# Neighbourhood attention by blocks of 16 columns in a two-block transformer kernel on one Trainium2 core

## The chip, the cores and the metric

The kernel runs on one core of a Trainium2 chip. The metric is the device time of one execution, in microseconds. The two kernels of this case are timed on the same chip, and a ratio of their times is read with its interval.

## What is computed

The reference is two transformer blocks. The change touches one part of the first: the attention layer over 512 latent tokens, seen as a grid of 8 rows by 64 columns, with 256 context tokens beside them. Its first half, neighbourhood attention, has 8 heads of 64 numbers. A latent query attends to the keys of a window of 8 rows by 16 columns around it, with a bias by relative position, and to all 256 context keys; since the grid has 8 rows, the window holds all of them, and only the columns slide. A context query attends to the context keys alone. Cut to what matters:

```python
row0 = clip(q_row - 4, 0, rows - 8)
col0 = clip(q_col - 8, 0, 64 - 16)
s_win = einsum('bqhd,bqkhd->bhqk', q, k[window]) * scale + rpb[:, rel_r, rel_c]
s_ctx = einsum('bqhd,bkhd->bhqk', q, k_ctx) * scale
p = softmax(concatenate([s_win, s_ctx], -1))
o = p[..., :128] @ v[window] + p[..., 128:] @ v_ctx
```

The result is gated by silu(ga), joined with that of a grouped-query attention (GQA), and multiplied by `w_out`. The rest of both blocks is the same in both kernels.

## The kernel before

The program is written once, in order, for all engines; a scheduler then lays out each engine's list, following the written order as a priority, and an engine runs its list in order. Work that is written as filler is mixed into the lists of the stage around it.

In `attn_layer` the projections come first. `gemm_T` gives an output turned (features on partitions, tokens along the row: `qaT`, `kaT`, `gaT`), in blocks of 256 features; `gemm_N` gives it natural (128 tokens on partitions), and makes `va`, six tiles of 128 tokens. Every product there is three products of rounded parts (lines 114 to 116).

Then comes the neighbourhood stage. `na_bias` loads `E`, for each query column the biases of all 64 key columns by 15 row distances, with eight loads, and adds a mask of -1e30 outside the window (line 463: the first two heads on VectorE, the others on GpSimd). `attend` runs over 4 head pairs `pr`, 3 query groups `qg` (two of 256 latent queries, one of context queries), 2 heads `p` and 2 tiles `i` of 128 queries, which are two grid rows. For a latent tile, `Softmax.probs` multiplies the queries with all 512 latent keys and with the 256 context keys (line 405, in two PSUM banks of the four `mm`), adds the bias and takes the maximum in one VectorE operation (line 414), reduces the second part (line 410), and runs two exponentials on ScalarE (line 420). `Softmax.transpose` turns the six tiles of 128 probabilities on TensorE (line 439), three to a bank of `tr`, and ScalarE and VectorE copy them out (lines 444 and 442). For a query group the six turned tiles are multiplied with `va` (line 751), the two heads innermost, each with its own half of the output's partitions. Lines 757 to 764 and `split` (199, 200) scale, gate and store the result. A matmul of 32-bit numbers stands in the trace as two passes.

`fill_a`, written ahead of head pair 0, is filler of this stage: it streams 32 pieces of 512 KB of modulation weights through two buffers and multiplies them (lines 333, 345, 369) in the one bank `fx`. The stage after it is the GQA, with filler `fill_b`.

Of the kernel before, what the change touches and what calls it, by code (L numbers as in the profile page):

```python
# [10 lines left out]
F32 = mybir.dt.float32  # L11
F32R = mybir.dt.float32r
AF = mybir.ActivationFunctionType
OP = mybir.AluOpType
# [434 lines left out]
NB = 64 * 15  # L449


def na_bias(b, pool, rpb, namask):


    nc = b.nc
    E = pool.tile([128, 8, 64, 15], F32, name="E")
    n = rpb.shape[1]
    for h in range(0, 8, 2):
        for a in range(2):
            src = bass.AP(tensor=rpb.tensor, offset=rpb.offset + h * n + 1 - a, ap=[[15, 64], [n, 2], [1, NB]])  # L460
            nc.sync.dma_start(E[64 * a:64 * a + 64, h:h + 2].rearrange("p h k x -> p h (k x)"), src)
        e = E[:, h:h + 2]
        (nc.gpsimd if h else nc.vector).tensor_tensor(e, e, namask[:, None, :, None].to_broadcast([128, 2, 64, 15]), op=OP.add)
    return E

# [61 lines left out]
def gemm_N(b, w, c0, ncols, hh, hl, nt, evac, tags=("mm", "ac"), done=None):  # L527
# [4 lines left out]
    ahead = []  # L532

# [42 lines left out]
def attn_layer(b, I, A, B, gates, modulate, consts, open_x, fill_a, fill_b):  # L576
# [29 lines left out]
    with b.banks(mm=4, tr=2, ac=2), tc.tile_pool(name="attn_h", bufs=1, side="right") as hp, \  # L606
# [21 lines left out]
        gemm_T(b, w_in, 0, 512, hh, hl, segs, put(qaT, lambda d, p: nc.scalar.activation(d, p, AF.Copy, scale=0.125)),  # L628
# [3 lines left out]
        qS, kS = gq.tile([128, 8, T], F32R, name="qS"), gq.tile([128, 2, 2, T], F32R, name="kS")  # L632
# [11 lines left out]
        for j in range(2):  # L644
            for cs in range(2):
# [82 lines left out]
    def attend(sm, pr, qT, kT, v, g2, bias, okt):  # L728


        for qg in range(3):
# [5 lines left out]
            for p in range(2):  # L737
                keys = lambda a, e: [k[:, a:e] for k in kT(p)]
                for i in range(2):
                    t = qg * 2 + i  # L740
                    q = qT(p)[:, t * 128:t * 128 + 128]
                    if lat and bias:
                        pieces = [(keys(0, 512), bias(2 * pr + p, t)), (keys(512, 768), None)]
                    else:
                        pieces = [(keys(0 if lat else 512, 768), None)]
                    pp = sm.probs(q, pieces, nk * 128, ri[:, i, p:p + 1])
# [5 lines left out]
            t = sm.work.tile([128, 256], F32, name="ot")  # L752
            sl = slice(qg * 256, qg * 256 + 256)

            rp = b.psum(256, sm.tags[1])
            rb = sm.work.tile([128, 4, 64], F32, name="ot")
            nc.gpsimd.tensor_scalar(rb, ri.rearrange("q i p -> q (i p)")[:, :, None].to_broadcast([128, 4, 64]), 1.0, 0.0,
                                    op0=OP.mult, op1=OP.add)
            for i in range(2):
                nc.tensor.transpose(rp[:, i * 128:i * 128 + 128],  # L760
                                    rb[:, 2 * i:2 * i + 2].rearrange("q p d -> q (p d)"), b.ident)
            nc.vector.tensor_mul(t, rp, g2[:, sl])
            nc.vector.scalar_tensor_tensor(t, o, 0.5, t, op0=OP.mult, op1=OP.mult)
            b.split(t, o_hi[okt // 4][:, okt % 4, sl], o_lo[okt // 4][:, okt % 4, sl])

    with b.banks(mm=4, tr=2, ac=1, fx=1), tc.tile_pool(name="na_e", bufs=1, side="right") as ep, \
            tc.tile_pool(name="na_w", bufs=2, side="right") as work:
        E = na_bias(b, ep, I["na_rpbP"], I["k_namask"])
        sm = Softmax(b, work)
        for pr in range(4):  # L770
            if pr == 0:
                fill_a("fx")
            attend(sm, pr, lambda p: qaT[64 * p:64 * p + 64, pr], lambda p: [kaT[64 * p:64 * p + 64, pr]],
                   lambda p, j: va[:, j, (2 * pr + p) * 64:(2 * pr + p) * 64 + 64], gaT[:, pr],
# [1753 lines left out]
```

## Time and profile before

| | us |
|---|---|
| median of 3 runs (2924.91 to 2933.57) | 2927.23 |
| the profiled execution | 2929.68 |
| its span, first to last instruction | 2927.9 |
| TensorE busy in the span | 2719.4 (93%) |
| VectorE / ScalarE / GpSimd busy | 1516.5 / 1035.1 / 511.9 |

The profile is of one execution. All durations below come from it; it lies 2.4 us above the median. PE is TensorE, PEld its weight loads, DVE VectorE, ACT ScalarE, POOL GpSimd. L405 is line 405. The windows view gives for a stretch (us from the span's start) its length, then for PE, PEld, DVE, ACT and POOL the busy time and the number of instructions that start in it, then TensorE's granted clock (1.00 is 2.4 GHz, 0.50 is 1.2 GHz), the DMA engines' busy share and the GB/s. A group of instructions stands as line, engine, operation, output<-inputs, shapes and count, then busy time in us and the mean of one in ns, then the idle time ahead of it and what ended that. For a matmul "64\*128" is rows by columns of the array that are in use and "64x512" the operand that streams through. The neighbourhood stage is the stretch from 281 to 462 us.

### The profile page before, as it was taken

To read this page: it belongs to the slowest core of one execution; us is meant where nothing else is said; L and a number is where in the kernel's file an instruction comes from. 1 tells how busy PE (TensorE), PEld (TensorE's weight loads), DVE (VectorE), ACT (ScalarE), POOL (GpSimd) and SP (SyncE) were. 2 spreads that over 40 slices of the span, in tenths; PEclk is the share of its full clock that TensorE was granted. 3 is DMA by queue.
4 is the path that set the end of the run, shared out by engine and by line. 5 is a ranking of instruction groups with operands and counts; after the bars stand their busy time and mean duration, and the time that the engine had idled before them with its cause. 6 is when DMAs were issued, how large, how long until landed. Compare 5 with 4: busy or idle time off the path is not lost. (4 is left out here: it accounts for less than half of the span.)

```text
span 2927.9 us, 43748 instructions
## 1 busy us (share of the span) xinstructions
PE 2719.4 (93%) x16874; PEld 2133.7 (73%) x16874; DVE 1516.5 (52%) x3218; ACT 1035.1 (35%) x2157; POOL 511.9 (17%) x803
## 2 busy tenths in 40 slices
PE   8998998989989889887999998999999998899998
PEld 5987445669767666667888877676878556888887
DVE  4144557645477788685434237662234445533423
ACT  3122336534444444213323224432224543322322
POOL 1011100221343332332000001311011333200000
PEclk9999899989889899988999998999999999999999
DMA  6112441132223322424333223223444114233322
GB/s 222 62 59 65 140 123 43 53 115 90 83 82 118 93 84 82 163 79 141 101 95 100 94 85 105 83 91 112 121 119 124 54 46 146 91 94 101 94 101 87
DMA packets 248796, 288.31 MB, mean 98 GB/s; under 512 B 16983, under 2 KB 196650, under 8 KB 248588
## 3 DMA queue, kind: packets, MB, share of 16 engines
q1 hardware_dynamic: 237068, 248.96, 27.2%
q0 software_dynamic: 10704, 33.41, 3.7%
q8 instruction: 133, 2.18, 0.3%
q10 hardware_dynamic: 816, 3.15, 0.3%
q14 instruction: 75, 0.61, 0.1%
HBM read 248.73 MB, written 35.68 MB: 97 GB/s over the span
## 5 line engine op out<-in xcount | busy, mean ns | idle before, releaser
L109 DVE TENSOR_TENSOR wlo<-wraw,whi 128x512 fp32r<-128x512 f32 (+1 forms) x390 | 368.6, 946 | 694.3 <-ACT whi L108 688.1
L108 ACT ACTIVATE whi<-wraw 128x512 fp32r<-128x512 f32 (+1 forms) x390 | 323.7, 831 | 809.6 <-PE mm L115 225.8
L114 PE MATMUL mm<-hh,whi 128*128 128x512 f32 (+1 forms) x992 | 371.8, 376 | 0.8 <-ACT hh L178 0.7
L115 PE MATMUL mm<-hl,whi 128*128 128x512 f32 (+1 forms) x992 | 371.8, 375 | 0.0
L116 PE MATMUL mm<-hh,wlo 128*128 128x512 f32 (+1 forms) x992 | 371.5, 375 | 0.1
L114 PEld LDWEIGHTS mm<-hh,whi 128*128 128x128 f32 x992 | 188.6, 191 | 34.2 <-ACT hh L178 1.3
L116 PEld LDWEIGHTS mm<-hh,wlo 128*128 128x128 f32 x992 | 188.4, 190 | 34.1 <-DVE wlo L109 1.2
L115 PEld LDWEIGHTS mm<-hl,whi 128*128 128x128 f32 x992 | 188.6, 190 | 32.2
L114 PE MATMUL mm<-whi,mh 128*128 128x512 f32 (+1 forms) x480 | 172.3, 360 | 1.4 <-DVE th L2138 1.4
L115 PE MATMUL mm<-wlo,mh 128*128 128x512 f32 (+1 forms) x480 | 173.2, 361 | 0.1
L116 PE MATMUL mm<-whi,ml 128*128 128x512 f32 (+1 forms) x480 | 172.8, 360 | 0.0
L114 PE MATMUL gt<-hh,whi 128*128 128x512 f32 (+1 forms) x320 | 128.4, 401 | 7.6 <-ACT whi L108 6.1
L116 PE MATMUL gt<-hh,wlo 128*128 128x512 f32 (+1 forms) x320 | 128.6, 402 | 0.6 <-DVE wlo L109 0.6
L115 PE MATMUL gt<-hl,whi 128*128 128x512 f32 (+1 forms) x320 | 127.8, 399 | 0.0
L283 POOL TENSOR_TENSOR ss<-sq 128x1 f32<-128x1 f32 x8 | 1.6, 201 | 708.0 <-ACT th L277 708.0
L114 PE MATMUL mm<-lath,whi 128*128 128x512 f32 (+1 forms) x280 | 117.7, 421 | 0.1
L116 PE MATMUL mm<-lath,wlo 128*128 128x512 f32 (+1 forms) x280 | 115.5, 413 | 0.6 <-DVE wlo L109 0.6
L115 PE MATMUL mm<-latl,whi 128*128 128x512 f32 (+1 forms) x280 | 115.2, 412 | 0.4 <-DVE latl L179 0.4
L114 PEld LDWEIGHTS mm<-whi,mh 128*128 128x128 f32 x480 | 89.9, 188 | 15.8 <-DVE th L2138 1.8
L115 PEld LDWEIGHTS mm<-wlo,mh 128*128 128x128 f32 x480 | 90.1, 188 | 14.6 <-DVE wlo L109 0.8
L116 PEld LDWEIGHTS mm<-whi,ml 128*128 128x128 f32 x480 | 90.1, 188 | 13.6
L439 PEld LDWEIGHTS tr<-ident,s 128*128 128x128 f32 x448 | 53.2, 148 | 52.6 <-ACT s L420 23.6
(716 smaller groups left out, 6157.0 us busy)
## 6 DMA issues: line engine op xcount, KB each, us to landing
wraw<-in_ffn_w_gate SPq DMA_DIRECT2D x44, 512.0 KB, 3.6
wraw<-in_ffn_w_up SPq DMA_DIRECT2D x44, 512.0 KB, 3.6
wraw<-in_ffn_w_down SPq DMA_DIRECT2D x44, 512.0 KB, 3.2
wraw<-in_w_in SPq DMA_DIRECT2D x60, 256.0 KB, 2.9
wraw<-in_rec_w_in SPq DMA_DIRECT2D x58, 256.0 KB, 2.8
wraw<-in_attn_w_in SPq DMA_DIRECT2D x26, 512.0 KB, 3.6
ada_w<-in_rec_ada_w SPq DMA_DIRECT2D x24, 512.0 KB, 3.9
wraw<-in_w_branch_gate SPq DMA_DIRECT2D x48, 256.0 KB, 3.0
```

Source lines behind the costliest of these rows:

```text
L108: nc.scalar.activation(hi, raw, AF.Copy)
L109: self.weng.tensor_sub(lo, raw, hi.bitcast(F32))
L114: mm(out, lh, rh, start=start, stop=False)
L115: mm(out, lh, rl, start=False, stop=False)
L116: mm(out, ll, rh, start=False, stop=stop)
L283: nc.gpsimd.tensor_add(ss, sq[:, i, 0:1], sq[:, i, 1:2])
L439: nc.tensor.transpose(t[:, j * 128:j * 128 + 128], p[:, (g + j) * 128:(g + j) * 128 + 128], b.ident)
```

## The change

The neighbourhood attention is cut another way. A query tile is a block of 16 columns by 8 rows instead of two grid rows, so its latent keys are a slice of columns of the grid: 32 columns (256 keys) for the two inner blocks and 24 columns (192 keys) for the two outer ones, instead of all 512. For this

- the evacuation of `qaT` writes the queries in the order block, column, row;
- the values are projected by `gemm_T` into `vT`, evacuated in groups of 8 columns by 8 rows, and turned by 24 transposes into `va` (`turn_v`, between the two halves of the gate's projection); `vT` stands in the buffer of `kS`, which is made after it;
- `E` is 8 row distances by 80 columns for each query and head, prepared ahead with the mask inside, loaded by eight loads; the mask's constant and the four additions are gone;
- the scores of the window and of the context go into one bank a head, and the products of the two heads alternate (`scores`);
- a tile has four tiles of probabilities to turn instead of six, in one bank; ScalarE copies two and VectorE two;
- the product with the values runs over four key tiles of 128 queries, instead of over six of 256;
- the gating reads `gaT` and writes the outputs in the grid's order, through views with a stride of 64 numbers.

The GQA keeps `attend`, of which the gating is now a function. Though the change's name also speaks of the sparse attention, no line of that is in the diff.

```diff
-NB = 64 * 15
+NA_E = 80
...
-    E = pool.tile([128, 8, 64, 15], F32, name="E")
...
+    E = pool.tile([128, 8, 8, NA_E], F32, name="E")
+    for h in range(8):
+        src = bass.AP(tensor=rpb.tensor, offset=rpb.offset + h * 16 * 15 * NA_E + 7 * NA_E,
+                      ap=[[15 * NA_E, 16], [-NA_E, 8], [1, 8 * NA_E]])
+        nc.sync.dma_start(E[:, h].rearrange("p r x -> p (r x)"), src)
...
+        def queries(j, ps):
+            d = qaT[:, j]
+            by = lambda x, how: x.rearrange(f"p ({how}) -> p r b c", b=4, c=16)
+            nc.scalar.activation(by(d[:, 0:S], "b c r"), by(ps[0], "r b c"), AF.Copy, scale=0.125)
+            nc.scalar.activation(d[:, S:T], ps[1], AF.Copy, scale=0.125)
...
-        gemm_N(b, w_in, 1024, 512, hh, hl, 6,
-               lambda c, i, p: nc.vector.tensor_copy(va[:, i, c * 256:c * 256 + 256], p))
-        gemm_T(b, w_in, 1536, 512, hh, hl, segs, put(gaT, lambda d, p: silu2(b, work, d, p)))
+        def values(j, ps):
+            v = vT[:, j]
+            grid = lambda x: x.rearrange("p (r c) -> p r c", c=64)
+            by = lambda x: grid(x)[:, :, 8:56].rearrange("p r (g c) -> p g r c", c=8)
+            nc.scalar.activation(v[:, 128:512].rearrange("p (g r c) -> p g r c", g=6, r=8), by(ps[0]), AF.Copy)
+            nc.vector.tensor_copy(v[:, 0:128].rearrange("p (g r c) -> p g r c", g=2, r=8),
+                                  grid(ps[0]).rearrange("p r (g c) -> p g r c", c=8)[:, ::7])
+            nc.scalar.activation(v[:, 512:768], ps[1], AF.Copy)
+        def turn_v(j):
+            v = vT[:, j]
+            for i, n in ((0, 4), (4, 2)):
+                p = b.psum(n * 128, "tr")
+                for m in range(n):
+                    nc.tensor.transpose(p[:, m * 128:m * 128 + 128], v[:, (i + m) * 128:(i + m) * 128 + 128], b.ident)
+                nc.vector.tensor_copy(va[:, i:i + n, j * 128:j * 128 + 128], p.rearrange("p (m f) -> p m f", m=n))
+        gemm_T(b, w_in, 1024, 512, hh, hl, segs, values)
+        gemm_T(b, w_in, 1536, 256, hh, hl, segs, put(gaT, lambda d, p: silu2(b, work, d, p)))
+        for j in range(4):
+            turn_v(j)
+        kS = gq.tile([128, 2, 2, T], F32R, name="kS")
+        gemm_T(b, w_in, 1536 + 256, 256, hh, hl, segs, put(gaT[:, 2:4], lambda d, p: silu2(b, work, d, p)))
...
+    def attend_na(sm, pr, E):
+        def scores(i):
+            ps = [b.psum(512, "mm") for _ in range(2)]
+            parts = [(256, [kaT[hs, pr, S:T] for hs in heads])]
+            if i < 4:
+                cols = slice(max(16 * i - 8, 0), min(16 * i + 24, 64))
+                n = 8 * (cols.stop - cols.start)
+                parts.insert(0, (n, [grid(kaT[hs, pr, 0:S])[:, :, cols] for hs in heads]))
+            o = 0
+            for n, ks in parts:
+                for p in range(2):
+                    nc.tensor.matmul(ps[p][:, o:o + n], qaT[heads[p], pr, 128 * i:128 * i + 128], ks[p], start=True, stop=True)
+                o += n
+            return ps, o
+        def probs(p, m, i, h, ri):
...
+            nc.vector.tensor_tensor_reduce(rows(z), rows(p), E[:, h, :, e0:e0 + w // 8], 1.0, NEG, OP.add, OP.max, mx[:, 0:1])
+            nc.vector.tensor_reduce(mx[:, 1:2], p[:, w:m], op=OP.max, axis=AX.X)
+            nc.vector.tensor_reduce(nm, mx, op=OP.max, axis=AX.X, negate=True)
+            nc.scalar.activation(s[:, 0:w].rearrange("p (g r c) -> p g r c", r=8, c=8),
+                                 z[:, 0:w].rearrange("p (r g c) -> p g r c", r=8, c=8), AF.Exp, bias=nm, accum_out=sums[:, 0:1])
+            nc.scalar.activation(s[:, w:m], p[:, w:m], AF.Exp, bias=nm, accum_out=sums[:, 1:2])
...
+            for x in range(2):
+                i = 2 * qg + x
+                ps, m = scores(i)
+                at = [0, m - 384] if lat else []
+                at += [m - 256, m - 128]
+                for p in range(2):
+                    s = probs(ps[p], m, i, 2 * pr + p, ri[:, x, p:p + 1])
+                    t = b.psum(512, "tr")
+                    for j, a in enumerate(at):
+                        nc.tensor.transpose(t[:, j * 128:j * 128 + 128], s[:, a:a + 128], b.ident)
+                    tv = t.rearrange("p (a b) -> p a b", b=128)
+                    xs = slice(128 * x, 128 * x + 128)
+                    nc.scalar.activation(pT[:, p, 0:2, xs], tv[:, 0:2], AF.Copy)
+                    if lat:
+                        nc.vector.tensor_copy(pT[:, p, 2:4, xs], tv[:, 2:4])
+            o = b.psum(256, "ac")
...
+                for j, (n, rows) in enumerate(tiles):
+                    for p in range(2):
+                        h = 2 * pr + p
+                        nc.tensor.matmul(o[heads[p], xs], va[rows, n, h * 64:h * 64 + 64], pT[rows, p, j, xs],
+                                         start=j == 0, stop=j == nk - 1)
+            gated(sm, o, ri, cut(gaT[:, pr]), cut(o_hi[0][:, pr]), cut(o_lo[0][:, pr]))
```

## Rows read from the trace of the kernel before

**Rows 1.** the page: the span and the busy time of TensorE.

```profile
span 2927.9 us, 43748 instructions
PE 2719.4 (93%) x16874; PEld 2133.7 (73%) x16874; DVE 1516.5 (52%) x3218; ACT 1035.1 (35%) x2157; POOL 511.9 (17%) x803
```

**Rows 2.** the windows view, by stretch: columns as in the section on the profile before.

```profile
281.00:292.00 11.00, 3.44 (x9) 1.91 (x10) 5.05 (x7) 0.38 (x1) 0.63 (x1) 0.81 0.91 222
292.00:312.00 20.00, 20.00 (x56) 9.84 (x56) 9.54 (x33) 7.85 (x24) 10.77 (x4) 0.51 0.70 167
312.00:462.00 150.00, 147.97 (x732) 66.21 (x728) 91.19 (x282) 58.79 (x182) 6.28 (x14) 1.00 0.35 108
466.00:600.00 134.00, 118.51 (x721) 83.71 (x722) 100.04 (x228) 80.74 (x183) 20.42 (x24) 0.96 0.19 63
```

**Rows 3.** groups of instructions by form, TensorE, 312 to 462 us.

```profile
L439 PE MATMUL tr<-ident,s 128*128 128x128 f32 x198 | 32.9, 285 | 0.7 <-DVE ot L762 0.4 <-ACT s L420 0.3
L751 PE MATMUL ac<-pT,va 128*64 128x256 f32 x202 | 32.5, 390 | 0.0
L405 PE MATMUL mm<-kaT,qaT 64*128 64x512 f32 x52 | 28.7, 631 | 0.0
L405 PE MATMUL mm<-kaT,qaT 64*128 64x256 f32 x86 | 27.9, 421 | 0.4 <-DVE mx L414 0.4
L760 PE MATMUL tr<-ident,ot 128*128 128x128 f32 x22 | 5.0, 303 | 0.2 <-POOL ot L757 0.2
L333 PE MATMUL fx<-ada_w,ada_cs 128*32 128x512 f32 x128 | 29.5, 605 | 0.7 <-DMA ada_w<-in_rec_ada_w 0.7
L369 PE MATMUL fx<-xt,k_sel 128*128 128x512 f32 x8 | 4.4, 632 | 0.0
L345 PE MATMUL fx<-k_sel,xt 128*128 128x2 f32 x32 | 4.2, 254 | 0.0
L369 PE MATMUL fx<-xt,k_sel 128*1 128x512 f32 x4 | 2.0, 591 | 0.0
```

**Rows 4.** TensorE: groups by form 435.24 to 435.30 us; three timeline pieces (start us, us, what).

```profile
L405 PE MATMUL mm<-kaT,qaT 64*128 64x512 f32 x1 | 0.7, 693 | 0.0
...
L405 PE MATMUL mm<-kaT,qaT 64*128 64x256 f32 x1 | 0.5, 480 | 0.0
...
435.24 0.70 PE L405 MATMUL mm<-kaT,qaT 64*128 64x256 f32 x2
...
444.81 0.44 PE L751 MATMUL ac<-pT,va 128*64 128x256 f32 x2
...
2392.58 1.09 PE L1923 MATMUL ac<-pT,vn 128*64 128x128 f32 x8
```

**Rows 5.** groups by form, VectorE and ScalarE, 312 to 462 us; last, line 1900 (ns min/median/max).

```profile
L414 DVE CUSTOM_DVE_ANT_1 s<-mm,E 128x512 f32<-128x512 f32 x26 | 27.4, 1052 | 7.8 <-PE mm L405 7.6
L442 DVE COPY pT<-tr 128x384 f32<-128x384 f32 x28 | 15.5, 552 | 6.5 <-PE tr L439 6.0
L410 DVE TENSOR_REDUCE mx<-mm 128x1 f32<-128x256 f32 x27 | 11.3, 419 | 2.8 <-PE mm L405 2.2
L420 ACT ACTIVATE s<-mm,nm 128x256 f32<-128x256 f32 x43 | 19.9, 464 | 2.6 <-DVE nm L408 2.1 <-DVE ri L425 0.5
L1900 DVE CUSTOM_DVE_ANT_0 s<-mm,E x96: 132/348/692, 2223.8 to 2431.4; 128x128 f32<-128x128 f32 x16, 128x256 f32<-128x256 f32 x16, 128x384 f32<-128x384 f32 x16, 128x512 f32<-128x512 f32 x16
```

**Rows 6.** timeline, the first biased tile; last, landing of the loads of E.

```profile
287.98 2.16 DVE L463 TENSOR_TENSOR E<-E,k_namask 128x1920 f32<-128x1920 f32 x1 [1.96 <-DMA E<-in_na_rpbP]
...
291.38 2.04 PE L405 MATMUL mm<-kaT,qaT 64*128 64x512 f32 x2 [7.21 <-DVE mx L414]
...
DMA to landing us min/median/max: 6.7/7.5/8.3
```

**Rows 7.** the windows view again, two blocks of 256 features: keys, then values.

```profile
85.36:102.04 16.68, 16.68 (x98) 14.76 (x97) 2.45 (x2) 3.86 (x6) 0.00 (x0) 1.00 0.21 64
127.78:145.06 17.28, 17.28 (x145) 17.28 (x144) 4.72 (x8) 2.12 (x2) 0.00 (x0) 1.00 0.20 62
```

More of the change, by code (lines that the diff above doesn't have):

```diff
@@ L446, in transpose, with na_bias @@
             g += m
-NB = 64 * 15
-def na_bias(b, pool, rpb, namask):
+NA_E = 80
+def na_bias(b, pool, rpb):
     nc = b.nc
-    E = pool.tile([128, 8, 64, 15], F32, name="E")
[L457 to L463, printed above, removed]
+    E = pool.tile([128, 8, 8, NA_E], F32, name="E")
[3 more added lines that the diff above has]
+        nc.sync.dma_start(E[:, h].rearrange("p r x -> p (r x)"), src)
     return E
@@ L627, in attn_layer @@
         modulate(work, place, ("tr", "tr"), 1)
[L628 removed]
+        def queries(j, ps):
[3 more added lines that the diff above has]
+            nc.scalar.activation(d[:, S:T], ps[1], AF.Copy, scale=0.125)
+        gemm_T(b, w_in, 0, 512, hh, hl, segs, queries,
                mid=lambda: half(1), pre=pre)
         consts()
[L632 removed]
+        qS, vT = gq.tile([128, 8, T], F32R, name="qS"), gq.tile([128, 4, T], F32, name="kS")
         kaT, gaT = na.tile([128, 4, T], F32, name="kaT"), na.tile([128, 4, T], F32, name="gaT")
@@ L726, in attn_layer, with attend @@
     open_o()
-    def attend(sm, pr, qT, kT, v, g2, bias, okt):
+    def attend(sm, pr, qT, kT, v, g2, okt):
         for qg in range(3):
@@ L741, in attend @@
                     q = qT(p)[:, t * 128:t * 128 + 128]
[L742 to L746, printed above, removed]
+                    pp = sm.probs(q, [(keys(0 if lat else 512, 768), None)], nk * 128, ri[:, i, p:p + 1])
                     sm.transpose(pp, pT[:, p, :, i * 128:i * 128 + 128], nk)
@@ L759, in attend @@
[L759 to L764, printed above, removed]
+            gated(sm, o, ri, g2[:, sl], o_hi[okt // 4][:, okt % 4, sl], o_lo[okt // 4][:, okt % 4, sl])
@@ new lines, in gated @@
+    def gated(sm, o, ri, g2, hi, lo):
+        rp = b.psum(256, sm.tags[1])
+        rb = sm.work.tile([128, 4, 64], F32, name="ot")
+        nc.gpsimd.tensor_scalar(rb, ri.rearrange("q i p -> q (i p)")[:, :, None].to_broadcast([128, 4, 64]), 1.0, 0.0,
+                                op0=OP.mult, op1=OP.add)
+        for i in range(2):
+            nc.tensor.transpose(rp[:, i * 128:i * 128 + 128],
+                                rb[:, 2 * i:2 * i + 2].rearrange("q p d -> q (p d)"), b.ident)
+        t = sm.work.tile([128, 256], F32, name="ot")
+        like = lambda x: x if len(g2.shape) == 2 else x.rearrange("p (b c r) -> p b c r", b=2, r=8)
+        nc.vector.tensor_mul(like(t), like(rp), g2)
+        nc.vector.scalar_tensor_tensor(t, o, 0.5, t, op0=OP.mult, op1=OP.mult)
+        b.split(like(t), hi, lo)
@@ L772, in attn_layer @@
                 fill_a("fx")
[L773 to L775 removed]
+            attend_na(sm, pr, E)
     right.close()
@@ L2408, in consts @@
     C["k_rope"] = np.stack([cos, sin], 0).reshape(2, 4, 128, 64).transpose(2, 0, 1, 3)
-    m = np.full((2, 64, 64), NEG)
-    for q in range(64):
-        c0 = min(max(q - 8, 0), 48)
-        m[:, q, 48 - c0:64 - c0] = 0
-    C["k_namask"] = m.reshape(128, 64)
     p = np.arange(128)
@@ L2469, in layout @@
     rpb = a["na_rpb"][0]
-    R["na_rpbP"] = np.zeros((8, 127 * 15 + 1), rpb.dtype)
-    R["na_rpbP"][:, 48 * 15:79 * 15] = rpb.transpose(0, 2, 1)[:, ::-1].reshape(8, -1)
+    parts = []
+    for q0, k0, n in ((16, 8, 32), (0, 0, 24), (48, 40, 24)):
+        t = np.full((8, 16, 15, n), NEG, rpb.dtype)
+        for q in range(q0, q0 + 16):
+            first = min(max(q - 8, 0), 48)
+            for k in range(max(k0, first), min(k0 + n, first + 16)):
+                t[:, q - q0, :, k - k0] = rpb[:, :, k - q + 15]
+        parts.append(t)
+    R["na_rpbP"] = np.concatenate(parts, 3).reshape(8, -1)
     R["ccols"] = np.stack([a["c"][0], a["c_ctx"]], -1).reshape(8, 128, 2).transpose(1, 0, 2)
```

47 lines of the change are left out of this document (37 added, 10 removed).

## The prediction

> **What bounds the kernel now.** The page comes first: TensorE is busy for 2719.4 of 2927.9 us [rows 1], so what counts is TensorE's own time, stage by stage. The windows view gives it for the neighbourhood stage, 281 to 462 us, 181 us long [rows 2]. Its body, 312 to 462, is TensorE's: 147.97 of 150 us busy at the full clock of 2.4 GHz, while VectorE is busy for 91.19 (61%) and ScalarE for 58.79. Its head is not: in 281 to 292 TensorE works 3.44 of 11 us, and after that idle stretch it runs at the lower clock (0.51) for 20 us, though it has work all the time. The gap ends when the first bias is masked and used: the mask takes VectorE 2.16 us after the load has landed, and TensorE's next scores wait 7.21 us for VectorE [rows 6]. So a pass taken from TensorE in the body is worth its time, as long as the others keep up. In the next stage, the GQA, they don't quite: VectorE is busy for 100.04 of 134 us (75%), and TensorE only for 118.51 (88%) [rows 2].
>
> **The price of a pass.** The groups by form give busy times in the body [rows 3]. Neighbouring groups overlap at their ends: the nine sum to 167.1 us and TensorE's busy time is 147.97, so each is taken at 0.885. That makes 0.147 us for a transpose (32.9 x 0.885 / 198), 0.142 for a pass of line 751, 0.488 and 0.287 for a score pass of 512 and 256 columns, 0.201 for one of line 760, and 35.5 for the filler (40.1 x 0.885). The whole stage has, by the code, 224 transposes, 224 passes of line 751, 64 and 96 score passes and 24 of line 760: 32.9 + 31.9 + 31.3 + 27.6 + 4.8 + 35.5 = 164.0 us. At the body's busy share of 0.987 this is 166.2; the remaining 14.8 of the 181 us are the head's idle time and lower clock.
>
> **Part by part, on TensorE.** *Transposes*: four instead of six for each of 32 latent tiles, two for 16 context tiles: 160 x 0.147 = 23.5 us, one answer. *Scores*: 128 passes of 256 columns and 32 of 192 (0.237 by the line through the two prices). One after the other they cost 36.7 + 7.6 = 44.3 us. But passes of two heads stand in different halves of the array's rows, and the trace has one such meeting: a pass of 512 and one of 256 columns are both over in 0.70 us, where the first alone takes 0.693 [rows 4]. The old order rarely brings that about (head by head), the new one writes it for every pair, so the lower end is half, 22.2. A pair can still be torn where the second bank isn't free in time; I take three in four as together, 27, nearer to the low end because line 751, written the same way, shows it: *the product with the values* has two heads' passes over in 0.44 us together where one has a mean of 0.390 [rows 4, 3]. It now has 320 passes of 128 columns. If each stood alone, the nearest row is line 1923, eight passes of this form in 1.09 us, 0.136 each [rows 4]: 43.6 us. If pairs stay as they are, half of 0.142 gives 22.8. I take 26, near the second, as the loop is the same one; what stands against it is that weight loads can bind short passes: in the values' block of the natural form (passes of 256 columns) they are busy for all of its 17.28 us, and it is longer than the block of the turned form for the same product [rows 7]. Line 760 and the filler stay: 4.8 and 35.5. The sum is 23.5 + 27 + 26 + 4.8 + 35.5 = 116.8 us, with ends of 108.8 and 151.7.
>
> **The other engines in the stage.** For a latent tile VectorE had 1.05 (bias, strided by 15 numbers) + 0.42 + 0.55 [rows 5] and small ones that stay. The bias is now half as long and contiguous: 0.53 if the old row is halved, 0.35 if the contiguous 0.692 of line 1900 is; the copy of 256 columns costs the 0.42 of line 410. That saves 0.65 to 0.83 us, 32 times, of nominal time; with the overlap of 0.87 that the body's VectorE groups show (91.19 busy against about 105 summed) about 20 us of the stage's 105.8. The gating of eight latent groups gets slower: three operations of 256 numbers through a stride of 64. The old strided row is 1.52 times the contiguous one (1052 against 692 ns), which adds 0.22 to each, 5 us in all; the least is nothing, and the most I put at four times the price, 30 us. So VectorE has some 88 us. [...] ScalarE has 1.4 us less in copies and exponentials for a tile and is not near its bound. GpSimd's three mask additions go; TensorE was busy all through them (20.00 of 20 us), so they are worth nothing [rows 2].
>
> VectorE's share then lies between the body's 61% and the GQA's 75%, and TensorE's busy share between 0.987 and 0.885. I take the middle, 0.93: 116.8 / 0.93 = 125.6 us. The head loses the mask (2.16 us) and a little of the load, whose first two pieces are smaller (6.7 to 8.3 us to landing now [rows 6]): 3 us, at least 2, at most 5. They leave SP's queue in the same place, between the gate's stores, which makes the later six late as before, but these belong to later head pairs. The lower clock after the gap stays, since a gap stays. The stage: 125.6 + 11.8 = 137.4, a gain of 43.6 us.
>
> **The projections.** A block of 256 features takes 17.28 us in the natural form and 16.68 in the turned one [rows 7]; two blocks gain 1.2. The 24 transposes cost 24 x 0.147 = 3.5. Net loss 2.3 us. They stand between the halves of the gate's projection, so what they wait for, the last evacuation of `vT`, is covered by a block of 16.68 us; behind them on TensorE stands the second half, and uncovered it would lose some 3 us. Their copies, and the evacuations of `vT`, fall where VectorE works 2.45 and ScalarE 3.86 of 16.68 us: hidden. The reordering of `qaT` is on ScalarE in such a block too: at double price still hidden. `kS` now waits for the last transpose, two blocks or more before its first use. Nothing of this has another answer.
>
> **The sum.** 43.6 - 2.3 = 41.3 us. The profiled execution would go from 2929.68 to 2888.4, the median from 2927.23 to 2886. The stages behind are TensorE's too and only start earlier, so I count nothing lost there.
>
> **Rivals.**
> *A, VectorE becomes the bound.* If the strided gating is at the upper price, VectorE has 113 us; at the 75% at which the GQA holds TensorE up, that is a stage of 151 us, and with some of the head 158: a gain of 23 - 2, some 2906. For it: TensorE gets faster and the evacuation hardly does. Against it: the old strided row is only 1.52. [...]
> *B, the heads don't overlap.* The scheduler tears the pairs, or short passes are held by their weight loads: 151.7 / 0.987 + 14.8 = 168.5, a gain of 12.5 - 2.3 = 10, 2917. Against it stand the two meetings of rows 4. This is also the case that the change doesn't do what it says.
> *C, slower: steps in a row.* A step is now both heads of a tile; two steps fill the four banks. If they don't overlap, each is scores 1.15 + VectorE 1.2 + two exponentials 0.93 [rows 5] + transposes 0.59 + copy 0.42 + the second head's turn 1.6 + values 1.3 = 7.2 us, and 24 of them with the filler and the head are 172 + 35.5 + 11.8 = 219, against 181: 2927 + 38 + 2 = 2967. It costs time from (181 - 2.3 - 35.5 - 11.8) / 24 = 5.5 us a step. Against it: the old stage kept TensorE at 0.987 with as many banks and a longer chain.
> *D, better*: all pairs together, TensorE at 0.987, the head 5 us shorter: 108.8 / 0.987 + 9.8 = 120, a gain of 61 - 2.3 = 59, 2868.
>
> **How the numbers follow.** Forecast 2886, 0.60 (2868 to 2905); A 0.16; B 0.12; C 0.05; D, below 2868, 0.07. The range from 2858 to 2918 holds all but C and the ends of B and D. A measurement of this kernel tells 0.3%, 8.8 us, from no change: faster is the forecast, A, D and most of B, 0.90; within 0.3% a part of B, 0.05; slower is C, 0.05.
>
> **What would show it.** In the new profile: score passes of two heads starting together, with the passes of 256 columns at about 0.17 us instead of 0.287; line 751's successor near 0.08 a pass; TensorE at 0.9 or more of a stage of some 137 us, with VectorE near 65%; the value blocks at 16.68 us; the first bias some 3 us earlier. The forecast is wrong if TensorE waits for VectorE in the stage (A), if the passes cost as much as they do alone (B), or if a step takes over 5.5 us (C).

## The result and the profile after

The changed kernel takes 2890.82 us (median of 4 runs, 2872.36 to 2898.25) against 2927.88 for the kernel before: a ratio of 0.986 [0.981, 0.991]. In a second series (`c1_changed_again` below) it was 2881.8 against 2922.4, 0.987 [0.985, 0.989]. The forecast was 2886 with 2858 to 2918, so the time came out as predicted; its parts did not, and they are the lesson. Executions of the changed kernel are spread over some 27 us, and the long ones are those with the lower granted clock (2870.6 us of span at 0.964, 2896.5 at 0.957). So below a stage is also given as its length times its granted clock, by estimate nearly what it would take at full clock (transposes of line 439 before followed each other at 0.213 us at a clock of 0.50 and at 0.109 at 1.00, in the median).

The page's second line and its span, answering [rows 1]:

```profile
span 2887.6 us, 43665 instructions
PE 2680.5 (93%) x16834; PEld 2113.6 (73%) x16834; DVE 1489.5 (52%) x3217; ACT 1030.0 (36%) x2165; POOL 501.7 (17%) x800
```

The windows view: first the whole stage, from its first score to the first score of the GQA stage, of before; then the same of after, then after's stretches that answer [rows 2], and one block of the values' projection for [rows 7]:

```profile
281.36:462.06 180.70, 171.46 (x792) 77.93 (x792) 105.62 (x320) 67.08 (x207) 17.69 (x19) 0.93 0.42 121
```

```profile
282.05:429.15 147.10, 141.04 (x813) 70.87 (x813) 77.27 (x316) 55.95 (x205) 7.60 (x16) 0.93 0.48 140
282.00:290.00 8.00, 5.73 (x30) 3.85 (x30) 4.07 (x22) 3.26 (x12) 0.63 (x1) 0.83 0.90 273
290.00:312.00 22.00, 22.00 (x105) 11.83 (x103) 9.54 (x43) 8.59 (x32) 0.82 (x2) 0.67 0.54 149
312.00:427.00 115.00, 111.17 (x662) 53.92 (x661) 62.73 (x249) 42.71 (x157) 5.75 (x12) 0.99 0.45 132
432.00:560.00 128.00, 114.23 (x702) 80.74 (x699) 95.11 (x217) 75.20 (x171) 19.67 (x23) 0.96 0.18 60
121.37:138.05 16.68, 16.68 (x97) 14.77 (x96) 3.03 (x4) 3.65 (x6) 0.00 (x0) 1.00 0.20 63
```

The stage went from 180.7 to 147.1 us, 33.6 less, both at a clock of 0.93; times clock it is 168.8 and 136.9 (clocks to three places). TensorE is busy for 96% of it, VectorE for 53%. So it is still TensorE's stage, as the forecast had it, but 10 us longer than the 137.4 forecast. Its groups of instructions, TensorE, 312 to 427 us, answering [rows 3]:

```profile
L333 PE MATMUL fx<-ada_w,ada_cs 128*32 128x512 f32 x118 | 29.9, 620 | 2.5 <-DMA ada_w<-in_rec_ada_w 1.3 <-DMA ada_w<-in_attn_ada_w 1.1
L813 PE MATMUL mm<-kaT,qaT 64*128 64x256 f32 x99 | 26.0, 422 | 0.0
L874 PE MATMUL ac<-pT,va 128*64 128x128 f32 x216 | 23.5, 287 | 0.0
L857 PE MATMUL tr<-ident,s 128*128 128x128 f32 x120 | 22.6, 293 | 1.4 <-ACT s L835 1.4
L813 PE MATMUL mm<-kaT,qaT 64*128 64x192 f32 x24 | 6.4, 366 | 0.0
L369 PE MATMUL fx<-xt,k_sel 128*128 128x512 f32 x8 | 4.5, 644 | 0.0
L787 PE MATMUL tr<-ident,ot 128*128 128x128 f32 x17 | 4.2, 307 | 0.0
L345 PE MATMUL fx<-k_sel,xt 128*128 128x2 f32 x32 | 4.1, 250 | 0.0
L874 PE MATMUL ac<-pT,va 64*64 64x128 f32 x24 | 3.9, 294 | 0.0
L369 PE MATMUL fx<-xt,k_sel 128*1 128x512 f32 x4 | 2.0, 590 | 0.0
```

By the prediction's own formula (these sum to 127.1, TensorE is busy for 111.17, so each times 0.875) a score pass costs 0.230 us, forecast 0.169; a pass of the values' product 0.100, forecast 0.081; a transpose 0.165, forecast 0.147. Why shows in the order of the passes, TensorE's timeline in after (start, length, line, shape, passes put together):

```profile
336.95 1.09 PE L874 MATMUL ac<-pT,va 128*64 128x128 f32 x16
337.97 1.07 PE L333 MATMUL fx<-ada_w,ada_cs 128*32 128x512 f32 x8
338.97 0.87 PE L874 MATMUL ac<-pT,va 128*64 128x128 f32 x10
...
342.92 1.05 PE L333 MATMUL fx<-ada_w,ada_cs 128*32 128x512 f32 x4 [1.32 <-DMA ada_w<-in_rec_ada_w]
343.90 0.66 PE L857 MATMUL tr<-ident,s 128*128 128x128 f32 x4
344.49 0.70 PE L813 MATMUL mm<-kaT,qaT 64*128 64x256 f32 x2
345.11 0.62 PE L333 MATMUL fx<-ada_w,ada_cs 128*32 128x512 f32 x2
```

Read the starts. Sixteen value passes, two heads side by side, take from 336.95 to 337.97: 1.02 us for eight pairs. Four transposes take 0.59 (343.90 to 344.49). In the experiment with pairs first, below, two transposes take 0.37 (342.03 to 342.40) before another form of work and 0.28 (339.96 to 340.24) before more transposes; eight value passes take 0.59. So a transpose or a pair of value passes adds 0.11 us, and a change to another form of passes some 0.15 on top (the form is the part of the array in use: 64\*128 for the scores, 128\*64 for the values, 128\*128 for transposes, 128\*32 for the filler). And line 813 at 344.49 is a torn pair: the two passes of *one* head, 0.62 us in which the other head's two could have run beside them. In the order of TensorE's instructions 42 of the stage's 80 score products stand next to one of the other head and 126 of the 160 value products; the work changes 205 times. Counted by form in the traces of the stage, there are 202 changes, against 176 before. Some of the 202 lie inside line 874, whose passes on half a key tile (64\*64) are a form of their own.

What happens at a change shows in the weight loads (PEld), first across two changes, then between two groups of transposes of one form, with the pass that the last load belongs to:

```profile
344.49 0.29 PEld L813 LDWEIGHTS mm<-kaT,qaT 64*128 64x128 f32 x2 [0.17 <-DVE mx L831]
345.11 0.14 PEld L333 LDWEIGHTS fx<-ada_w,ada_cs 128*32 128x32 f32 x4 [0.33 <-issue]
...
428.90 0.25 PEld L857 LDWEIGHTS tr<-ident,s 128*128 128x128 f32 x2
429.01 0.38 PE L857 MATMUL tr<-ident,s 128*128 128x128 f32 x2
```

Within a form the load starts about one pass ahead of its pass (428.90 and 429.01; in the median of the stage's 559 such passes at full clock 0.108 us ahead, though 78 start within 3 ns of their load; before, 0.213). Across a change it starts together with it (344.49 and 345.11, the starts of the passes above). That holds for all 202 changes of the stage, and for all 176 before, within 3 ns. So in both stages TensorE loaded no weights ahead across a change of form. Nor is the gap a wait for another engine: from the last transpose to the first pass of the scores, the values or the filler it is 0.203 us in the median of each (16, 13 and 9 cases at full clock), where transposes follow each other at 0.109. How much of the 0.15 us is the late load is not shown.

The forecast's price of a pass held the cost of the changes. It was multiplied by the number of passes, and halved for pairs. But the changes did not get cheaper or fewer with smaller passes: 202 x 0.148 is some 30 us of the stage, and 176 x 0.148 was 26 before.

### The profile page after: what moved, and what is told of

The parts are those of the page before. It is cut to its first block, busy times and chain, and to the rows that moved or that the text cites. A ratio compares the mean times of both kernels' runs of the same rounds, so it can differ in the third digit from the quotient of the medians.

```text
span 2887.6 us, 43665 instructions
## 1 busy us (share of the span) xinstructions
PE 2680.5 (93%) x16834; PEld 2113.6 (73%) x16834; DVE 1489.5 (52%) x3217; ACT 1030.0 (36%) x2165; POOL 501.7 (17%) x800
## 5 line engine op out<-in xcount | busy, mean ns | idle before, releaser
L114 PE MATMUL mm<-hh,whi 128*128 128x512 f32 (+1 forms) x1024 | 384.2, 376 | 0.8 <-ACT hh L178 0.7
L115 PE MATMUL mm<-hl,whi 128*128 128x512 f32 (+1 forms) x1024 | 383.7, 375 | 0.0
L116 PE MATMUL mm<-hh,wlo 128*128 128x512 f32 (+1 forms) x1024 | 383.4, 375 | 0.0
L115 PE MATMUL mm<-latl,whi 128*128 128x512 f32 (+1 forms) x280 | 114.0, 407 | 0.4 <-DVE latl L179 0.4
L114 PEld LDWEIGHTS gt<-hh,whi 128*128 128x128 f32 x320 | 61.6, 193 | 21.1 <-ACT whi L108 6.7
```

Of the source, the lines that this page charges most:

```text
L114: mm(out, lh, rh, start=start, stop=False)
L115: mm(out, lh, rl, start=False, stop=False)
L116: mm(out, ll, rh, start=False, stop=stop)
```

## The experiments

**Theory.** TensorE's own time sets the stage: so many slots (a pair of passes, or a lone one, costs the same) plus some 0.16 us for each change of work (the expectations' figure; the rows above give 0.15). **Rivals.** VectorE's longer gating sets the pace; the heads don't overlap; the chain through VectorE and ScalarE sets it and TensorE's changes only fill waiting time. All runs below are versions of the changed kernel. The table holds each run's median, its ratio to the kernel before on the same chip, the stage (first score to first GQA score), its granted clock and product, and from the order of the instructions the changes of work, the scores in pairs (of 80) and the values in pairs (of 160).

```
run                         us      ratio [interval]       stage  clock  product  changes scores values
after                       2890.8  0.986 [0.981, 0.991]   147.1  0.930  136.9    205     42     126
c1_changed_again            2881.8  0.987 [0.985, 0.989]   146.2  0.942  137.7    205     42     126
e1_heads_apart              2897.8  0.994 [0.992, 0.996]   164.4  0.907  149.0    219     34      50
e2_gate_flat                2886.9  0.990 [0.988, 0.992]   150.0  0.909  136.4    205     42     126
e3_one_tile_per_pair        2911.3  0.997 [0.996, 0.999]   169.2  0.862  145.9    224     36     128
e4_pair_first               2862.0  0.982 [0.980, 0.984]   121.9  0.986  120.2    154     80     138
e5_values_apart             2893.6  0.991 [0.988, 0.994]   160.4  0.936  150.2    210     42      54
e6_filler_four              2878.9  0.986 [0.983, 0.990]   148.7  0.805  119.6    186     38     130
e11_filler_four_again       2868.2  0.982 [0.979, 0.984]   130.2  0.948  123.4    186     38     130
e7_pair_first_filler_four   2858.3  0.979 [0.976, 0.981]   119.3  0.955  114.0    139     80     138
e8_filler_four_later        2874.6  0.983 [0.979, 0.986]   146.9  0.849  124.7    189     48     132
e9_pair_first_filler_later  2855.4  0.976 [0.973, 0.980]   115.4  0.956  110.3    141     80     138
e10_no_filler               2838.4  0.972 [0.969, 0.975]    96.3  1.000   96.3    171     36     128
```

The product is good to some 4 us where clocks differ much: the same kernel gave 119.6 at 0.805 and 123.4 at 0.948. It comes from one execution a row, but the whole execution's span times its mean clock, averaged over all runs of a kernel, says much the same: 2795 and 2796 us before, 2765 and 2769 for the changed kernel, 2776 and 2781 with heads or values apart, 2778 with one tile per pair, 2752 with pairs first, 2757 (twice) with the filler by four and 2756 with it later, 2742 and 2744 for both together, 2723 without filler.

The theory can be set against the traces. An estimate: each slot at its spacing inside a group of passes (0.109 us for 128 columns, 0.216 for 256, 0.433 for 512, 192 in proportion) and 0.148 us for each change of form, counted from the starts in the stage; beside it TensorE's busy time times the clock.

```
run                      slots    changes of form     sum     busy x clock
before                   133.1    176 = 26.0          159.1   160.1
after                    100.5    202 = 29.9          130.4   131.2
e1_heads_apart           110.7    228 = 33.7          144.4   143.9
e4_pair_first             88.3    141 = 20.9          109.2   112.3
e6_filler_four            87.6    180 = 26.6          114.2   115.7
e10_no_filler             65.0    168 = 24.9           89.9    94.1
```

Two prices thus give TensorE's work within 5% in six orders of the work. The changed kernel itself, a second time:

> The changed kernel itself, a second time, as the measure for the runs beside it. Its stage from the first score to the first score of the next stage was 147.1 us at a granted clock of 0.93, 136.8 us when multiplied: the product should come within 1.5 us of that, whatever the clock does, if TensorE bounds the stage, while the stage itself may move by as much as the clock. If the product moves with the stage's length the theory that TensorE's work sets it is wrong.

137.7 against 136.9, with a clock of 0.942 for 0.930: the product is a fair measure.

**Heads apart** (scores and values), what the turns are worth:

```diff
-            o = 0
-            for n, ks in parts:
-                for p in range(2):
+            for p in range(2):
+                o = 0
+                for n, ks in parts:
...
-                for j, (n, rows) in enumerate(tiles):
-                    for p in range(2):
+                for p in range(2):
+                    for j, (n, rows) in enumerate(tiles):
```

> The change kept, but in the scores and in the product with the values all passes of one head are issued before those of the other. In the order of TensorE's instructions 50 of the 160 value products stand next to one of the other head instead of 126, and 34 of the 80 score products instead of 42; the changes from one kind of work to another go from 205 to 219. Theory (TensorE is the bound, two passes side by side cost one, and a change of work about 0.16 us): 38 more value slots of two passes of 0.109 us = 8.3 us, 4 more score slots of 0.43 us = 1.7 us, 14 changes = 2.2 us: the stage some 12 us longer than the 147.1 us of the changed kernel, about 2903 us in all. Rival (the heads never overlapped, so the turns are worth nothing): within 2 us. Rival (the prediction's price of no overlap): 31 us longer.

The second hunk alone:

> The change kept; only the product with the values issues all passes of one head before those of the other, the scores stay in turns. In TensorE's order 54 of 160 value products stand next to the other head's instead of 126; changes of work 210 instead of 205. Theory: 36 more slots of two passes of 0.109 us = 7.8 us and 5 changes of 0.16 us = 0.8 us: stage times clock 145.4 us instead of 136.8. Rival (the values product hides beside other work, the first experiment's loss came from the scores): within 2 us of 136.8.

The whole stage of the first, then of the second:

```profile
281.38:445.74 164.36, 158.71 (x830) 81.50 (x831) 80.70 (x321) 56.67 (x208) 7.30 (x16) 0.91 0.42 125
```

```profile
281.77:442.20 160.43, 153.31 (x836) 80.17 (x837) 81.97 (x321) 56.69 (x209) 7.71 (x17) 0.94 0.43 129
```

Products of 149.0 and 150.2 against 136.9: the turns are worth some 12 us, so the heads do overlap, and within the 4 us of the measure all of it lies in the values. In the scores, as the change writes them, the turns are worth nothing that shows: with heads apart 34 of 80 still meet, against 42. (The second expectation, 145.4, was 5 us low.) It also splits the change: from 149.0 to 136.9, 12 us, is the turns; from 168.8 to 149.0, 20 us, is all the rest, the smaller blocks and some 5 us less idle time at the head.

**The gate without its turn** (output positions mixed up):

```diff
-            gated(sm, o, ri, cut(gaT[:, pr]), cut(o_hi[0][:, pr]), cut(o_lo[0][:, pr]))
+            flat = lambda a: a[:, 256 * qg:256 * qg + 256]
+            gated(sm, o, ri, flat(gaT[:, pr]), flat(o_hi[0][:, pr]), flat(o_lo[0][:, pr]))
```

> The change kept, but the gate factors of the stage are read and its result is written without the turn from blocks of 16 columns into rows, so the positions of the attention output are mixed up: the strided reads and writes of VectorE are gone, 12 times about 0.16 + 0.10 + 0.19 us = 5.4 us of VectorE time. Theory (TensorE bounds the stage at 96% busy): stage 147 us within 1.5 us. Rival (VectorE's longer work sets the pace): some 4 to 5.5 us shorter.

VectorE's three operations of one latent group, which go through the stride in after, and the same group in this run:

```profile
340.24 0.59 DVE L791 TENSOR_TENSOR ot<-tr,gaT 128x256 f32<-128x256 f32 x1 [2.49 <-PE tr L787]
341.89 0.37 DVE L199 CAST oh<-ot 128x256 fp32r<-128x256 f32 x1
342.49 0.60 DVE L200 TENSOR_TENSOR ol<-ot,oh 128x256 fp32r<-128x256 f32 x1
```

```profile
341.13 0.42 DVE L791 TENSOR_TENSOR ot<-tr,gaT 128x256 f32<-128x256 f32 x1 [2.50 <-PE tr L787]
342.78 0.28 DVE L199 CAST oh<-ot 128x256 fp32r<-128x256 f32 x1
343.38 0.42 DVE L200 TENSOR_TENSOR ol<-ot,oh 128x256 fp32r<-128x256 f32 x1
```

The stride costs VectorE 0.09 to 0.18 us an operation, 1.3 to 1.4 times, or some 3.5 us over the eight latent groups. It costs the stage nothing: a product of 136.4 against 136.9 (the length, 150.0, missed the expectation by the clock, 0.909). That ends rival A.

**Pairs kept together.** First only one tile for both heads' scores, then with a higher priority for the scores, so that nothing is set between the two heads:

```diff
-            ps = [b.psum(512, "mm") for _ in range(2)]
+            both = b.mm2.tile([128, 1024], F32, name="mm2")
+            ps = [both[:, 512 * p:512 * p + 512] for p in range(2)]
...
                 for p in range(2):
+                  with tc.high_priority(offset=5000):
                     nc.tensor.matmul(ps[p][:, o:o + n], ...
...
-    with b.banks(mm=4, tr=2, ac=1, fx=1), ...
+    with b.banks(mm2=2, tr=2, ac=1, fx=1), ...
```

> The change kept, but the scores of both heads of a block lie in one PSUM tile of two banks (two such tiles) where there were four tiles of one bank. Nothing else changes, but the order that comes of it has 224 changes of work on TensorE instead of 205, and 36 of 80 score products next to the other head's instead of 42. Theory (changes cost 0.16 us): 19 changes = 3.0 us, 3 more score slots = 1.3 us: stage about 4 us longer, 151 us. Rival (the number of changes costs nothing; what counts is that both heads' banks come free together): 0 to 3 us shorter.

> As the run before it, with the score products of this stage given a higher priority than all else, so that both heads' passes stand together: 80 of 80 in pairs, 154 changes of work instead of 205; passes, shapes and the other engines' work are the same. Theory: 19 score slots of 0.43 us = 8.2 us and 51 changes of 0.16 us = 8.2 us: stage 16 us shorter than 147.1, so 131 us, and about 2875 us in all. Rival (VectorE's and ScalarE's chain from scores to exponentials to transposes sets the pace, TensorE's changes are waiting time in disguise): stage within 3 us of 147, with TensorE idle where it had been busy. Rival (scores that run ahead hold the banks): 3 to 8 us longer.

The second: the whole stage, and a piece of TensorE's timeline:

```profile
279.68:401.62 121.94, 113.89 (x812) 60.67 (x813) 77.21 (x317) 55.13 (x205) 7.73 (x16) 0.99 0.55 169
```

```profile
339.96 0.44 PE L787 MATMUL tr<-ident,ot 128*128 128x128 f32 x2
340.24 0.38 PE L859 MATMUL tr<-ident,s 128*128 128x128 f32 x2
...
342.03 0.44 PE L859 MATMUL tr<-ident,s 128*128 128x128 f32 x2
342.40 0.66 PE L876 MATMUL ac<-pT,va 128*64 128x128 f32 x8
342.99 1.13 PE L815 MATMUL mm<-kaT,qaT 64*128 64x256 f32 x8
344.05 1.07 PE L333 MATMUL fx<-ada_w,ada_cs 128*32 128x512 f32 x8
```

One tile per pair without the priority made it worse, by 9 us where 4 was expected: it added changes, and TensorE's idle time grew from 6.1 to 9.2 us. With the priority the same passes take 120.2 against 136.9, 16.7 us less, where the theory said 16 and the rivals 0 to 3 or a loss. At 342.99 eight score passes of both heads take 1.06 us, where two of one head alone took 0.62 in after. The chain through VectorE and ScalarE had not set the pace: they did the same work (77.2 and 55.1 us) in a stage 25 us shorter. No run tried pairs and changes apart; by the count above 12 us less are slots and 9 less are changes, and TensorE waits some 2 us more.

**The filler by four.**

```diff
-        for kb in range(4):
+        kk = 0
+        while kk < 8:
             w = place()
+            m = w.shape[1]
...
-                    place = lambda: pool.tile([128, 2, 512], F32, name="ada_w", bufs=2)
+                    place = lambda: pool.tile([128, 4, 512], F32, name="ada_w", bufs=2)
```

> The change kept; the filler between the attention's passes (the adaptive-norm product) loads four blocks of weights in one transfer of 1 MB instead of two in 512 KB, so that its passes on the four column groups of TensorE stand together: 15 runs of filler instead of 30, 186 changes of work instead of 205, the same products. Theory: a run of two or of four filler products takes the same 0.97 us or so, so 15 runs less is about 14 us, with 1 us given back in scores (38 of 80 in pairs instead of 42): stage times clock about 124 us instead of 136.8. Rival (the loads pace the filler, and larger loads land later): 0 to 5 us. Rival (the filler fills TensorE's waits and costs nothing): 0, with TensorE idle instead.

> The one-tile pairs with scores first and the filler by four together: 80 of 80 score products in pairs, 17 runs of filler, 139 changes of work instead of 205. Theory: 16 us and 13 us add up: stage times clock about 108 us instead of 136.8, total some 40 us under the changed kernel's. Rival (another engine takes over as the bound: VectorE was busy 77 us and ScalarE 55 us of the stage, and the chain from scores through the exponential to the transposes is a wait for each block): the sum is not reached, stage times clock 113 to 121 us with TensorE idle for more than 10 us in it.

The timeline of after shows why it was tried: eight filler passes on four column groups take 1.00 us (337.97 to 338.97), four on two groups 0.98 (342.92 to 343.90). The products fell as expected and a little more (119.6 and, the second time, 123.4). But the first profile's stage was 148.65 us, no shorter than without. The windows of that profile, and what stood ahead on TensorE; the waiting row's bracket is idle time and its releaser:

```profile
370.00:377.50 7.50, 5.92 (x41) 3.08 (x39) 6.08 (x27) 2.85 (x11) 0.00 (x0) 1.00 0.00 0
377.50:421.90 44.40, 44.08 (x181) 25.38 (x180) 18.73 (x78) 14.46 (x53) 1.52 (x4) 0.50 0.00 1
...
375.28 0.44 PE L859 MATMUL tr<-ident,s 128*128 128x128 f32 x2 [1.56 <-ACT s L837]
```

The clock fell to its lower level, 0.50, at 377.5, 9 us after the filler's last product with the weights and 6 after its last small pass, and stayed there for 44.4 us, with TensorE busy for 44.08 of them. A theory formed on that: the filler holds the clock up. Three runs were to tell: the filler by four but begun with the third pair of heads (`if pr == 2:` for `if pr == 0:` before `fill_a`), the kernel without a filler, and the same kernel again.

> As the run with the filler by four, where the filler's last pass stood at 368 us and the granted clock fell to half from 377.5 us for 44.4 us; here the filler begins with the third pair of heads instead of the first, so that the same 16 runs of filler are spread to the end of the stage (17 runs, 189 changes of work against 186, 48 instead of 38 of 80 score products in pairs). Theory (with the filler gone the remaining passes do not hold the clock, and that alone gave the saved 17 us back): no low stretch of 44 us, stage times clock again about 118 us, and the stage some 126 to 132 us instead of 148.6. Rival (the clock fell for something the filler does not touch, such as what ran before the stage): the low stretch stays, the stage stays above 140 us. Rival (a late filler holds the next stage up): the stage is short, and the lead is lost before 600 us.

> The change kept, with the filler left out: its results (the gates and the second layer's norm factors) are set to a constant, so the numbers behind it are not the reference's. 160 passes of the filler's products and 44 of its small passes are gone from TensorE, 40 us of the stage's 147; the attention's own passes stay, 171 changes of work. Theory by TensorE's work: stage times clock about 100 us instead of 136.9. If the granted clock stays at full speed but for the first 15 us, the stage is 105 to 110 us. Theory that the filler keeps the clock up: low stretches of 40 us and more, stage 120 to 145 us at the same product. Rival (the chain through VectorE and ScalarE was hidden by the filler): stage times clock 110 us or more with TensorE idle for over 10 us.

```diff
-                    ad.gates(pool, place, 2, gates, (tag, tag))
-                    ar.modulation(pool, place, I["rec_norm_c"], rc["A"], rc["B"], (tag, tag))
-                    ar.gates(pool, place, 1, rgate, (tag, tag))
+                    for x in (gates, rc["A"], rc["B"]):
+                        nc.gpsimd.memset(x, 0.5)
+                    row = pool.tile([1, 1024], F32, name="row")
+                    nc.gpsimd.memset(row, 0.5)
+                    nc.sync.dma_start(rgate, row)
```

> The filler by four once more, to see whether its low stretch of 44.4 us after the filler's end at 368 us returns at the same place. Theory (it belongs to the order of the work): a low stretch of 20 us or more begins within 15 us of the filler's end, stage times clock 119.6 us within 1.5, stage over 138 us. Rival (it falls where it likes): no such stretch there, stage 120 to 135 us at the same product.

The filler later, its low stretch:

```profile
371.50:392.00 20.50, 20.50 (x88) 9.37 (x86) 6.83 (x23) 4.83 (x19) 0.80 (x2) 0.50 0.35 118
```

The stage without filler; then the filler by four again, the stretch after the filler's end and the same kind of wait:

```profile
279.46:375.75 96.29, 94.13 (x640) 56.04 (x641) 67.03 (x296) 54.99 (x205) 6.03 (x13) 1.00 0.12 34
```

```profile
367.40:409.26 41.86, 38.79 (x270) 22.68 (x262) 28.09 (x118) 21.73 (x81) 2.19 (x5) 1.00 0.01 3
...
374.21 0.89 PE L859 MATMUL tr<-ident,s 128*128 128x128 f32 x4 [1.56 <-ACT s L837]
```

The theory fell. Without any filler the clock stayed at full for the whole stage; with the filler spread there was still a low stretch of 20.5 us at 371.5, while filler ran; and the same kernel, with the same wait of 1.56 us at the same place, kept the full clock the second time. So in these runs the low stretches do not follow from the order of the work; what sets them stays open. The run without filler does bear out the sum: 96.3 us, where 100 was expected, so the filler's 40 us are paid in full on TensorE (this kernel leaves out the filler's work on the other engines and its loads too).

**Both, with the filler later:**

> One-tile pairs with scores first, the filler by four and beginning with the third pair of heads: 80 of 80 score products in pairs, 19 runs of filler, 141 changes of work against 139. With the filler early this had 119.3 us of stage at a granted clock of 0.955, 114.0 us multiplied, TensorE idle 12.5 us of it, most of it before value products after the filler had ended. Theory (the filler spread to the end fills those waits and holds the clock): TensorE idle under 8 us, stage times clock 108 to 111 us, stage 111 to 116 us, total 4 to 8 us under that run's ratio of 0.9786, so about 0.976. Rival (VectorE's and ScalarE's chain sets the pace once TensorE is relieved): idle stays above 12 us, no change beyond 2 us.

```profile
279.16:394.59 115.43, 107.59 (x812) 60.92 (x813) 76.66 (x317) 55.00 (x205) 7.67 (x16) 0.96 0.55 178
```

With the filler early (e7) the two savings did not add up: a product of 114.0 instead of 108, with 12.5 us idle on TensorE, so there the rival's numbers were met: TensorE waited for the other engines. With the filler begun later it is 110.3 and 7.8 idle, as the theory said. At 2855.4 us, a ratio of 0.976 [0.973, 0.980], this version beats both kernels: about 1% under the changed one, whose interval ends at 0.985.

## Why the prediction was right, and where not

*TensorE bounds the stage.* Right: 96% busy (0.93 was taken), and the gate's stride cost nothing. Rivals A and C are out: nothing ran in steps, and VectorE was busy for 77.3 us where 88 were reckoned. The bias was 0.34 to 0.43 us, at the low end, and the gating's stride cost 1.3 to 1.4 times, not 1.52.

*The price of a pass.* This is the step that failed. With 0.230, 0.100 and 0.165 us (0.233 for the 192 columns) the stage's passes make 36.9 for the scores (27 forecast), 32.0 for the values (26) and 26.4 for the transposes (23.5); with 5.2 for the small transposes and some 37.7 for the filler it is 138.2 us instead of 116.8. TensorE's busy time times the clock says it without a formula: it fell from 160 to 131 us, by 29, where the forecast's sums fell from 164.0 to 116.8, by 47. The largest miss is the scores. "Three in four together" was 42 of 80, which by 0.43 us a lone product is 4 of the 10 us. The rest of the miss is put down to the changes of form, which the price per pass had hidden: the forecast let their share shrink with the passes, and it grew from 26 to 30 us.

*What made up for it.* Three terms, two of them in the stage. The busy share: 138.2 / 0.967 is 142.9, which adds 4.7 us of idle time where 8.8 were forecast. The head: by this sum 4 us are left for it, where 11.8 were forecast. Its own rows give more: 2.3 us idle, and 22 us at a clock of 0.67, which loses 7.3; the same count gives 17.4 before (7.6 and 9.8), so the head gained some 8 us where 3 were forecast. So the 138.2 is some 5 us too high; 24 of the stage's 836 passes, about 3 us, stand behind the GQA's first score. The head had been cut by more than the mask. The loads of `E` landed in 4.0/4.7/5.4 us, against 6.7/7.5/8.3 [rows 6], and the first biased scores stood 5.8 us earlier, not 3. VectorE's timeline, before and then after:

```profile
290.17 1.05 DVE L414 CUSTOM_DVE_ANT_1 s<-mm,E 128x512 f32<-128x512 f32 x1
```

```profile
284.41 0.36 DVE L831 CUSTOM_DVE_ANT_1 sb<-mm,E 128x192 f32<-128x192 f32 x1 [2.51 <-DMA E<-in_na_rpbP]
```

TensorE was idle for 2.3 of the first 8 us (7.6 of 11 before), and the low stretch behind it had a clock of 0.67 over 22 us instead of 0.51 over 20. That a gap brings a low stretch, as the forecast took it, is not shown: from 279 to 312 us `e4_pair_first` had TensorE idle for 5.2 us at a clock of 0.95, after for 4.0 us at 0.74.

*The projections.* The value blocks are 16.68 us, as forecast. The stage began 0.7 us later than before, against the 2.3 forecast; but the same kernel in `c1_changed_again` began it at 279.52, 1.8 us earlier than before, so a difference of this size can't be read from one execution.

*The end.* The stage and what lies ahead of it account for 32.9 us (462.06 to 429.15, the GQA's first score); the profiled executions differ by 40.3. The other 7 came later, where nothing was changed and the forecast counted nothing. TensorE's busy share in the GQA is as before (89%, 88% in [rows 2]), but the mean granted clock of the whole run was 0.959 against 0.955. At full clock the part outside the stage would even have been 6 us longer (2633.3 against 2626.9 us of span times clock, while its length was 2740.5 against 2747.2). So the 7 us are the clock, and luck: nothing in the forecast spoke of it. Over all runs it is the same: at full clock the change saves 26 to 31 us (2795 and 2796 against 2765 and 2769), and in the second series a mean clock of 0.960 against 0.957 gives another 8. No run shows that the change raised the clock: with the gate flat, on another chip, it was 0.9585 against 0.9581. So the forecast's gain of 41.3 us and the profiled 40.3 (37.1 by the medians) agree by compensation: TensorE's passes gave 18 us less than forecast, and the busy share, the head and the clock gave most of it back.

*B, that the heads don't overlap,* was right for the scores as scheduled and wrong for the values. Its price (168.5 us) was not put to the test: with both apart the stage was 164.4 us, at a clock of 0.907, but 34 score and 50 value products still met.

## What to carry to other kernels

Price TensorE's work from starts, not from busy sums: slots of passes that run side by side, plus a fixed cost for each change between forms of work (here 0.148 us); then ask how many changes the schedule leaves, since smaller passes did not make them fewer (202 after, 176 before). Writing two heads in turns did not make them neighbours in TensorE's order (42 of 80 score products); look there, and tie them (one tile, one priority) if they are not. And compare a stage's length times its granted clock before explaining a difference of some tens of us (148.7 and 130.2 us for the filler by four twice, 119.6 and 123.4 multiplied).

## What the runs showed of the hardware that was not expected

A change between forms of passes (64\*128, 128\*64, 128\*128, 128\*32) cost some 0.15 us here (transposes 0.59 us for four, of which 4 x 0.109 are slots). From one line's transposes to another's, of the same form, it was about 0.09 less (0.28 us against 0.37 for two). Across a change of form the first weight load started together with its pass, in all 202 cases of the stage; within a form it started 0.108 us ahead in the median of 559. Filler passes on four column groups of 32 took no longer than on two (eight passes in 1.00 us, four in 0.98). TensorE was busy for 44.08 of 44.40 us at the lower clock of 0.50 (`e6_filler_four`), at a place where the same kernel in another execution had 1.00 (`e11_filler_four_again`). At a clock of 0.50 the passes of 512 columns of lines 114 to 116 before started every 0.427 us, at 1.00 every 0.227 us (medians), which is 1.2 and 2.3 columns a ns. Taken as one column a cycle, an estimate, the 0.427 us make the 1.2 GHz that stands ahead for 0.50, and so 2.4 for 1.00. VectorE's operations of 128x256 with operands through a stride of 64 numbers took 0.59, 0.37 and 0.60 us against 0.42, 0.28 and 0.42.
